# Small TensorE products that merge triangular inverses: order by head and then by block, two groups' 64-row steps alternating, and block transposes as 32x32 products

## The chip, the cores and the metric

The kernel runs on one core of a Trainium2 chip. The core has a matrix engine (TensorE, here PE, with its weight loads shown as a row of their own, PEld), a vector engine (VectorE, DVE), an engine for activations and copies (ScalarE, ACT), a general engine (GpSimd, POOL) and an engine that issues most of the transfers (SyncE, SP). The engines run their own instruction lists and wait for each other by semaphores. Matrix products are written to PSUM, the accumulators' memory; everything else lies in SBUF. The metric is the device time of one execution in microseconds; the median of three executions is given.

## The reference

Two decoder layers on 256 tokens of width 1024, all in float32. Each layer is a gated feed-forward part, a token mixer and a second feed-forward part, each between two RMS normalisations and added to the stream. The mixer runs a gated delta rule (8 heads of width 128, chunks of 64 tokens) beside a causal convolution of 31 taps. What matters here is the delta rule's triangular system:

```python
kk = jnp.einsum("bhncd,bhnsd->bhncs", k, k)
a_mat = jnp.where(strict, kk * decay * beta[..., :, None], 0.0)
lhs = jnp.eye(CHUNK, dtype=jnp.float32) + a_mat
rhs = jnp.concatenate([v * beta[..., None], k * (beta * jnp.exp(G))[..., None]], axis=-1)
sol = lax.linalg.triangular_solve(lhs, rhs, left_side=True, lower=True, unit_diagonal=True)
```

`lhs` is unit triangular. The kernel does not solve with it, it forms its inverse (over blocks of 128 tokens, so two blocks for each of 8 heads) and multiplies.

## The kernel before, in words

**Large products.** Every dense product is done in three parts, high·high, high·low and low·high, from weights that are split on the chip: a piece of weights is loaded into `raw` (four buffers), ACT rounds it to `whi` and DVE or POOL subtracts to get `wlo` (eight buffers each). These products write `mm` and make up most of PE's list. They come as a stream with the names `mm<-whi,xt`, `mm<-wlo,xt`, `mm<-whi,xt`.

**What sets the order.** PE's list is the order in which the program is written. Inside the mixer's projection a planner (`Lanes`) counts ticks of three or six large products each; small jobs (generators that yield between their steps) are put between the large products when their delay, in ticks, is over (`DELAY`, one number for each step of a job; the last one is used for all that follow). The planner also keeps a rough clock for PE, DVE and POOL, and gives a `wlo` subtraction to POOL or to DVE by those clocks. So a job with one step fewer, or with products of another counted cost, can move what comes behind it.

**The merge.** The inverse is built in blocks of 32 rows: POOL works out the inverses of the four 32x32 diagonal blocks of each matrix by substitution (`inverse`), transfers bring them into `U` (tile `u`). The job `merge` then puts the blocks together. A tile `u` or `at` holds 8 matrices of 128x128, 4 heads times 2 token blocks (the index `th`); there are two groups of heads (`gp` 1 and 0), so 16 matrices in all. The steps, with a yield after each:

- T, four times: four transposes of 128x128 into one PSUM tile, then three ACT copies of diagonal 32x32 blocks into `at`.
- A, for each group: 8 products of 32x32 for block 0, then 8 for block 64.
- B, for each group: 8 for block 0 and 8 for block 64 (named `gd<-u,at`), then 8 more for rows 32 to 64 (`gd<-at,u`).
- C, for each group: 8 products of 64x64 that contract over rows 0 to 64 and write rows 64 to 128 (`gd<-at`).
- D, for each group: 8 products of 64x64 that contract over rows 64 to 128 and write rows 0 to 64 (`gd<-u,at`).

Behind each step ACT copies the result to SBUF, and a later step waits for that copy. In every step six or nine large products stand between one block of small ones and the next. When `merge` is done the scan (`scan_first`, blocks `gd<-vr,u` and on) may begin. All small float32 products appear in the trace as two passes, each a weight load and a product; a 128x128 transpose is one pass. The trace's line L144 is the helper that issues products, L150 the one that issues transposes, L171 all of ACT, L124 all of DVE and POOL.

**Which rows a product uses.** PE's array takes the contracted rows from the partitions where the operands lie, and writes the partitions where the output lies. In A the two blocks use rows 0 to 32 with output 32 to 64, and rows 64 to 96 with output 96 to 128. In B they use rows 32 to 64 with output 0 to 32, rows 96 to 128 with output 64 to 96, and for the third kind rows 32 to 64 with output 32 to 64.

Of the kernel before, what the change touches and what calls it, by code (L numbers as in the profile page):

```python
# [12 lines left out]
AF = mybir.ActivationFunctionType  # L13
ALU = mybir.AluOpType

P = 128
# [315 lines left out]
def trunk(ctx: ExitStack, tc: tile.TileContext, x_in, wfirst, consts, feat, pch, tokp,  # L332
# [29 lines left out]
    def ps_gd(shape=None):  # L362
        return psum.tile(shape or [P, 4, P], F32, name="gd", tag="tr", bufs=3)
# [3 lines left out]
    T = Products(nc.tensor)  # L367
    V, S, W = Clocked(nc.vector, vector_us), Held(nc.scalar, T), Clocked(nc.gpsimd, pool_us)
# [29 lines left out]
    ident = cst[:, K_ID:K_ID + P]  # L398
# [345 lines left out]
    def mixer(xt, l, after_mix):  # L744
# [214 lines left out]
        AT = [None, None]  # L959
        U = [None, None]  # L960
# [62 lines left out]
        def merge():  # L1023
            ps = [None, None]
            for gp in (1, 0):
                at = AT[gp]
                for tb in range(2):
                    ts = slice(tb * 4, tb * 4 + 4)
                    pt = ps_gd()
                    for hl in range(4):  # L1030
                        T.transpose(pt[:, hl, :], U[gp][:, tb * 4 + hl, :], ident)
                    for b in (0, 64, 32):
                        S.copy(at[b:b + 32, ts, b:b + 32], pt[b:b + 32, :, b:b + 32])
                    yield
            for gp in (1, 0):
                at, ps[gp] = AT[gp], ps_gd([P, 16, 32])
                for b in (0, 64):
                    for th in range(8):
                        T.matmul(ps[gp][b + 32:b + 64, th, :], at[b:b + 32, th, b + 32:b + 64], at[b:b + 32, th, b:b + 32],
                                 start=True, stop=True)  # L1040
                for b in (0, 64):
                    S.copy(at[b + 32:b + 64, :, b:b + 32], ps[gp][b + 32:b + 64, 0:8, :])
                W.memset(at[0:32, :, 32:64], 0.0)
                yield
            for gp in (1, 0):
                at, u, p = AT[gp], U[gp], ps[gp]
                for b in (0, 64):
                    for th in range(8):
                        T.matmul(p[b:b + 32, 8 + th, :], at[b + 32:b + 64, th, b:b + 32], u[b + 32:b + 64, th, b + 32:b + 64],
                                 start=True, stop=True)  # L1050
                for th in range(8):
                    T.matmul(p[32:64, 8 + th, :], u[32:64, th, 32:64], at[32:64, th, 0:32], start=True, stop=True)
                for b in (0, 64):
                    S.activation(u[b:b + 32, :, b + 32:b + 64], p[b:b + 32, 8:16, :], AF.Copy, scale=-1.0)
                S.activation(at[32:64, :, 0:32], p[32:64, 8:16, :], AF.Copy, scale=-1.0)
                yield
            for gp in (1, 0):
                at, ps[gp] = AT[gp], ps_gd([P, 8, 64])
                for th in range(8):
                    T.matmul(ps[gp][64:128, th, :], at[0:64, th, 64:128], at[0:64, th, 0:64], start=True, stop=True)  # L1060
                S.copy(at[64:128, :, 0:64], ps[gp][64:128])
                yield
            for gp in (1, 0):
                at, u = AT[gp], U[gp]
                for th in range(8):
                    T.matmul(ps[gp][0:64, th, :], at[64:128, th, 0:64], u[64:128, th, 64:128], start=True, stop=True)
                S.activation(u[0:64, :, 64:128], ps[gp][0:64], AF.Copy, scale=-1.0)
                yield

        vr = [None, None]  # L1070

# [144 lines left out]
        def take(c):  # L1216
# [17 lines left out]

        acts = {
            "f": take, "decays": lambda c: decays(), "dts": lambda c: decay_pairs(), "inv": lambda c: inverse(), "merge": lambda c: merge(),
            "qs": lambda c: q_scale(), "cn": lambda c: conv_norm(), "cn1": lambda c: conv_out(1), "on": lambda c: o_norm(), "on0": lambda c: o_first(),
            "s0": lambda c: scan_first(), "s1": lambda c: scan_second(),
# [268 lines left out]
```

## Time and profile before

| | |
|---|---|
| median of 3 executions | 1353.26 us (1352.9 to 1353.55) |
| profiled execution, first to last instruction | 1349.7 us, so 3.56 us less than the median |
| PE busy | 98% of the span |
| granted TensorE clock | 0.999 |
| merge in layer 1, first to last small block | 352.3 to 381.5 us |
| merge in layer 2 | 1019.7 to 1049.2 us |

A row of the timeline gives the start, the time from the first start to the last end, the engine, the line, the operation, the tiles it writes and reads, and how many instructions were merged into the row. A matmul's end is modelled, and matmuls overlap, so what a block takes is read from starts: from the last large product ahead of it to the second large product behind it (the first one behind a block starts early and its successor is late), less two steps of the large products' pace.

### The profile page before, as it was taken

The numbers are of one execution on the slowest core, as the hardware profiler recorded it, in microseconds if no ns is written. First come the engines' busy times: TensorE is split into PE (matmuls) and PEld (weight loads), VectorE is DVE, ScalarE is ACT, GpSimd is POOL, SyncE is SP. The second block draws the span as 40 slices with busy tenths as digits, with TensorE's granted clock in tenths as the row PEclk, the third lists the DMA queues.
The fourth block names the chain that finished last, engine by engine and source line by source line (L and its number), as shares of the span: only waits on it lengthen the run. The fifth ranks groups of instructions, "written<-read, shape, count | busy, mean of one in ns | idle before, by whom it ended". The sixth has DMA issues, their size and how long they took to land.

```text
span 1349.7 us, 20220 instructions
## 1 busy us (share of the span) xinstructions
PE 1327.1 (98%) x7259; PEld 1128.0 (84%) x7259; DVE 933.8 (69%) x1594; ACT 732.3 (54%) x1175; POOL 445.5 (33%) x374
## 2 busy tenths in 40 slices
PE   9999999999999999999999999999999999999998
PEld 7888889997787888888888888899977878888886
DVE  6676455999966776665576654579999666766553
ACT  7545447675555545544455543577656564555541
POOL 0111017798744201111011120277986431011110
PEclk9999999999999999999999999999999999999999
DMA  8878746562634666776468775465545446477861
GB/s 274 287 239 260 249 156 210 166 211 96 206 110 153 225 218 222 276 249 221 155 219 280 265 235 186 146 231 172 173 138 183 143 139 234 154 261 247 273 212 39
DMA packets 115652, 273.76 MB, mean 203 GB/s; under 512 B 24768, under 2 KB 48352, under 8 KB 115552
## 3 DMA queue, kind: packets, MB, share of 16 engines
q1 hardware_dynamic: 115264, 272.40, 61.5%
q8 instruction: 57, 0.93, 0.3%
q14 instruction: 43, 0.35, 0.1%
q10 hardware_dynamic: 288, 0.07, 0.0%
HBM read 256.68 MB, written 15.75 MB: 202 GB/s over the span
## 4 chain that ended last, share of the span: by engine, by line
PE 81%; DVE 11%; ACT 3%; DMA 2%; issue 1%; POOL 1%; DVEq 0%; POOLq 0%; SPq 0%; ACTq 0%
PE mm L144 75%; DVE cacc L124 4%; PE gd L144 3%; DVE c L124 3%; DVE wlo L124 2%; PE tr L150 2%; DMA raw<-mw 2%; ACT whi L171 1%; DVE at L124 1%; ACT dt L171 1%; ACT sg L171 0%; DMA raw<-w2i 0%; DVE ssk L124 0%; DVE qk L124 0%; POOL rk L124 0%
## 5 line engine op out<-in xcount | busy, mean ns | idle before, releaser
L144 PE MATMUL mm<-whi,xt 128*128 128x512 f32 (+1 forms) x2048 | 647.6, 391 | 3.0 <-ACT qT L171 2.2
L171 ACT CAST whi<-raw 128x1024 fp32r<-128x1024 f32 (+2 forms) x448 | 458.8, 1035 | 316.8 <-PE mm L144 173.8
L124 DVE TENSOR_TENSOR wlo<-raw,whi 128x1024 fp32r<-128x1024 f32 (+2 forms) x342 | 427.2, 1264 | 190.0 <-ACT whi L171 183.5
L144 PEld LDWEIGHTS mm<-whi,xt 128*128 128x128 f32 x2048 | 382.3, 188 | 82.3 <-ACT qT L171 3.0
L144 PE MATMUL mm<-wlo,xt 128*128 128x512 f32 (+1 forms) x1024 | 396.4, 387 | 0.1
L124 POOL TENSOR_TENSOR wlo<-raw,whi 128x1024 fp32r<-128x1024 f32 (+1 forms) x106 | 250.5, 2379 | 142.5 <-ACT whi L171 140.0
L144 PEld LDWEIGHTS mm<-wlo,xt 128*128 128x128 f32 x1024 | 192.6, 188 | 37.6 <-DVE wlo L124 1.3
L144 PE MATMUL mm<-whi,act 128*128 128x512 f32 x704 | 218.3, 390 | 0.0
L124 POOL TENSOR_TENSOR act<-way,act 128x512 fp32r<-128x512 f32 x44 | 79.1, 1798 | 396.1 <-ACT act L171 385.9
L124 DVE SCALAR_TENSOR_TENSOR cacc<-hT,pc,cacc 128x254 f32<-128x254 f32 (+28 forms) x464 | 179.5, 472 | 0.2
L144 PE MATMUL mm<-xt,whi 128*128 128x256 f32 x960 | 175.5, 285 | 0.8 <-ACT qT L171 0.6
L144 PEld LDWEIGHTS mm<-whi,act 128*128 128x128 f32 x704 | 132.2, 188 | 27.4
L144 PEld LDWEIGHTS mm<-xt,whi 128*128 128x128 f32 x960 | 149.4, 192 | 1.9 <-ACT qT L171 0.9
L144 PE MATMUL mm<-wlo,act 128*128 128x512 f32 x352 | 137.0, 389 | 0.0
L144 PE MATMUL mm<-xt,wlo 128*128 128x256 f32 x480 | 135.9, 283 | 0.0
L171 ACT ACTIVATE ag<-mm,rstd 128x256 f32<-128x256 f32 x88 | 41.7, 474 | 100.0 <-PE mm L144 80.5
L144 PEld LDWEIGHTS mm<-xt,wlo 128*128 128x128 f32 x480 | 92.0, 192 | 0.0
L124 DVE SCALAR_TENSOR_TENSOR ag<-mm,rstd,ag 128x256 f32<-128x256 f32 x88 | 42.3, 481 | 58.7 <-ACT ag L171 58.4
L144 PEld LDWEIGHTS mm<-wlo,act 128*128 128x128 f32 x352 | 66.1, 188 | 13.6
L124 POOL TENSOR_TENSOR rpost<-ss,exp 128x1 f32<-128x1 f32 x12 | 6.5, 538 | 193.8 <-DVE ss L124 193.8
L171 ACT ACTIVATE jk<-mm 128x512 f32<-128x512 f32 x24 | 14.3, 598 | 60.4 <-PE mm L144 60.4
L124 DVE SCALAR_TENSOR_TENSOR c<-mm,pc,c 128x255 f32<-128x255 f32 (+2 forms) x108 | 43.7, 478 | 2.6 <-ACT c L171 2.6
(187 smaller groups left out, 1148.3 us busy)
## 6 DMA issues: line engine op xcount, KB each, us to landing
raw<-mw SPq DMA_DIRECT2D x168, 512.0 KB, 3.8
raw<-w2i SPq DMA_DIRECT2D x88, 512.0 KB, 4.8
raw<-w1i SPq DMA_DIRECT2D x84, 512.0 KB, 4.9
raw<-w1o SPq DMA_DIRECT2D x44, 512.0 KB, 4.7
raw<-w2o SPq DMA_DIRECT2D x44, 512.0 KB, 4.3
way<-way SPq DMA_DIRECT2D x176, 64.0 KB, 1.8
way<-way SPq DMA_DIRECT2D x44, 256.0 KB, 4.8
wbc<-feat SPq DMA_DIRECT2D x13, 512.0 KB, 4.9
```

The lines of the kernel that those rows point to most:

```text
L124: r = op(out, *a, **k)
L144: r = self.eng.matmul(o, w, x, **k)
L150: r = self.eng.transpose(*a)
L171: r = op(*a, **k)
```

## The change

Three edits in `merge`, nothing else:

- T: the four 128x128 transposes of a step become twelve products of a 32x32 diagonal block with the 32x32 identity (`gd<-cst,u`, line 144 now). The blocks are 0, 64 and 32 for each head in turn. The fourth diagonal block was never copied, and isn't made any more.
- A and B: the loops are swapped, so that for each matrix the products of all blocks follow each other; in B the third kind goes into the same loop.
- C and D: group 1's C stands alone as before. Group 0's C and group 1's D become one step in which their products alternate, followed by both ACT copies; group 0's D stands alone. Four steps become three.

```diff
                     for hl in range(4):
-                        T.transpose(pt[:, hl, :], U[gp][:, tb * 4 + hl, :], ident)
+                        for b in (0, 64, 32):
+                            bs = slice(b, b + 32)
+                            T.matmul(pt[bs, hl, bs], U[gp][bs, tb * 4 + hl, bs], ident[bs, bs], start=True, stop=True)
...
-                for b in (0, 64):
-                    for th in range(8):
+                for th in range(8):
+                    for b in (0, 64):
                         T.matmul(ps[gp][b + 32:b + 64, th, :], at[b:b + 32, th, b + 32:b + 64], at[b:b + 32, th, b:b + 32],
                                  start=True, stop=True)
...
-                for b in (0, 64):
-                    for th in range(8):
+                for th in range(8):
+                    for b in (0, 64):
                         T.matmul(p[b:b + 32, 8 + th, :], at[b + 32:b + 64, th, b:b + 32], u[b + 32:b + 64, th, b + 32:b + 64],
                                  start=True, stop=True)
-                for th in range(8):
                     T.matmul(p[32:64, 8 + th, :], u[32:64, th, 32:64], at[32:64, th, 0:32], start=True, stop=True)
...
-            for gp in (1, 0):
-                at, ps[gp] = AT[gp], ps_gd([P, 8, 64])
-                for th in range(8):
-                    T.matmul(ps[gp][64:128, th, :], at[0:64, th, 64:128], at[0:64, th, 0:64], start=True, stop=True)
-                S.copy(at[64:128, :, 0:64], ps[gp][64:128])
-                yield
-            for gp in (1, 0):
-                at, u = AT[gp], U[gp]
-                for th in range(8):
-                    T.matmul(ps[gp][0:64, th, :], at[64:128, th, 0:64], u[64:128, th, 64:128], start=True, stop=True)
-                S.activation(u[0:64, :, 64:128], ps[gp][0:64], AF.Copy, scale=-1.0)
-                yield
+
+            def inner(gp, th):
+                T.matmul(ps[gp][64:128, th, :], AT[gp][0:64, th, 64:128], AT[gp][0:64, th, 0:64], start=True, stop=True)
+
+            def outer(gp, th):
+                T.matmul(ps[gp][0:64, th, :], AT[gp][64:128, th, 0:64], U[gp][64:128, th, 64:128], start=True, stop=True)
+
+            ps[1] = ps_gd([P, 8, 64])
+            for th in range(8):
+                inner(1, th)
+            S.copy(AT[1][64:128, :, 0:64], ps[1][64:128])
+            yield
+            ps[0] = ps_gd([P, 8, 64])
+            for th in range(8):
+                inner(0, th)
+                outer(1, th)
+            S.copy(AT[0][64:128, :, 0:64], ps[0][64:128])
+            S.activation(U[1][0:64, :, 64:128], ps[1][0:64], AF.Copy, scale=-1.0)
+            yield
+            for th in range(8):
+                outer(0, th)
+            S.activation(U[0][0:64, :, 64:128], ps[0][0:64], AF.Copy, scale=-1.0)
+            yield
```

How the rows on PE moved is shown at three places; a count behind a row is how many instructions stand there. First a T step of layer 1, PE's list before:

```order
L144 MATMUL mm<-whi,xt 128x512
L150 MATMUL gd<-cst,u 128x128 x4
L144 MATMUL mm<-whi,xt 128x512
L144 MATMUL mm<-wlo,xt 128x512
L144 MATMUL mm<-whi,xt 128x512 x2
```

and now:

```order
L144 MATMUL mm<-whi,xt 128x512
L144 MATMUL gd<-cst,u 32x32 x12
L144 MATMUL mm<-whi,xt 128x512
L144 MATMUL mm<-wlo,xt 128x512
L144 MATMUL mm<-whi,xt 128x512 x2
```

Twelve small products stand where four transposes stood; the large products around them are the same. Second, step B of group 1, PE's list before:

```order
L144 MATMUL mm<-whi,xt 128x512
L144 MATMUL gd<-u,at 32x32 x16
L144 MATMUL gd<-at,u 32x32 x8
L144 MATMUL mm<-whi,xt 128x512
L144 MATMUL mm<-wlo,xt 128x512
```

and now (the first two of eight matrices):

```order
L144 MATMUL mm<-whi,xt 128x512
L144 MATMUL gd<-u,at 32x32 x2
L144 MATMUL gd<-at,u 32x32
L144 MATMUL gd<-u,at 32x32 x2
L144 MATMUL gd<-at,u 32x32
```

The 24 products are the same and stand between the same large products; only their order differs. Third, group 0's C and group 1's D on PE, before:

```order
L144 MATMUL gd<-at 64x64 x8
L144 MATMUL mm<-whi,xt 128x512
L144 MATMUL mm<-wlo,xt 128x512
L144 MATMUL mm<-whi,xt 128x512 x2
L144 MATMUL mm<-wlo,xt 128x512
L144 MATMUL mm<-whi,xt 128x512
L144 MATMUL gd<-u,at 64x64 x8
```

and now (the first two of eight pairs, and the large product ahead of them):

```order
L144 MATMUL mm<-whi,xt 128x512
L144 MATMUL gd<-at 64x64
L144 MATMUL gd<-u,at 64x64
L144 MATMUL gd<-at 64x64
L144 MATMUL gd<-u,at 64x64
```

The six large products that stood between the two blocks now come after the pair, so all that follows `merge` stands six large products earlier in PE's list, up to the transposes of the convolution's result, where the six come back. The planner also gives one `wlo` subtraction of each layer, near the merge, to POOL instead of DVE; ACT's list has the same instructions with some casts and copies exchanged.

## The prediction

> **What bounds the kernel now.** I read the page first, then the chain of waits around the merge, then PE's timeline there.
>
> ```profile
> span 1349.7 us, 20220 instructions
> PE 1327.1 (98%) x7259; PEld 1128.0 (84%) x7259; DVE 933.8 (69%) x1594; ACT 732.3 (54%) x1175; POOL 445.5 (33%) x374
> PE 81%; DVE 11%; ACT 3%; DMA 2%; issue 1%; POOL 1%; DVEq 0%; POOLq 0%; SPq 0%; ACTq 0%
> ```
>
> PE is busy nearly always and makes up 81% of the chain that ends last. In layer 1 the chain from the first transposes of the merge to well behind the scan is PE alone:
>
> ```profile
> 352.32 0.66 PE gd L150 x4
> ...
> 407.31 2.73 PE mm L144 x12
> ```
>
> All pieces between these two, too, are PE's small blocks and large products in turn. So here what a block of small products takes from PE is what it adds to the time, until a stall further on swallows it. The chain does not say how long a block takes by itself, so I read prices from the timeline's starts.
>
> **The pace and the price of each block.** A T step:
>
> ```profile
> 354.67 0.40 PE L144 MATMUL mm<-whi,xt 128*128 128x512 f32 x1
> 354.90 0.60 PE L150 MATMUL gd<-cst,u 128*128 128x128 f32 x4
> 355.26 0.48 PE L144 MATMUL mm<-whi,xt 128*128 128x512 f32 x1
> 355.57 0.39 PE L144 MATMUL mm<-wlo,xt 128*128 128x512 f32 x1
> 355.81 0.61 PE L144 MATMUL mm<-whi,xt 128*128 128x512 f32 x2
> 356.26 0.39 PE L144 MATMUL mm<-wlo,xt 128*128 128x512 f32 x1
> ```
>
> Three large products take 356.26 - 355.57 = 0.69, so 0.23 each. From the large product ahead to the second behind: 355.57 - 354.67 = 0.90, less two paces 0.46: **T costs 0.44**. Step A of group 1:
>
> ```profile
> 360.15 0.40 PE L144 MATMUL mm<-whi,xt 128*128 128x512 f32 x1
> 360.48 1.09 PE L144 MATMUL gd<-at 32*32 32x32 f32 x32
> 361.50 0.50 PE L144 MATMUL mm<-whi,xt 128*128 128x512 f32 x1
> 361.83 0.40 PE L144 MATMUL mm<-wlo,xt 128*128 128x512 f32 x1
> ```
>
> and of the view of the tile `gd`, with the least, median and greatest duration in ns:
>
> ```profile
> L144 PE MATMUL gd<-at x192: 191/191/267, 360.5 to 1043.7; 32*32 32x32 f32 x128, 64*64 64x64 f32 x64
> ```
>
> 1.68 - 0.46: **A costs 1.22**. That row (all products named so) gives 0.19 for one pass's own duration, so the 32 passes' starts cover 1.09 - 0.19 = 0.90, and 0.32 of the price is getting into the block and out of it. Step B of group 1 is the row that decides most:
>
> ```profile
> 366.07 0.40 PE L144 MATMUL mm<-whi,xt 128*128 128x512 f32 x1
> 366.40 1.00 PE L144 MATMUL gd<-u,at 32*32 32x32 f32 x29
> 367.21 0.21 PE L144 MATMUL gd<-at,u 32*32 32x32 f32 x1
> 367.24 0.19 PE L144 MATMUL gd<-u,at 32*32 32x32 f32 x1
> 367.26 0.19 PE L144 MATMUL gd<-at,u 32*32 32x32 f32 x1
> 367.27 0.19 PE L144 MATMUL gd<-u,at 32*32 32x32 f32 x1
> 367.29 0.19 PE L144 MATMUL gd<-at,u 32*32 32x32 f32 x1
> 367.30 0.19 PE L144 MATMUL gd<-u,at 32*32 32x32 f32 x1
> 367.32 0.57 PE L144 MATMUL gd<-at,u 32*32 32x32 f32 x13
> 368.17 0.40 PE L144 MATMUL mm<-wlo,xt 128*128 128x512 f32 x1
> ```
>
> 2.10 - 0.46: **B costs 1.64**. The thirteen passes at the end start every (0.57 - 0.19) / 12 = 0.032: one place of the array takes a pass every 0.032. But where the kind changes, the first `at,u` passes start while three `u,at` passes are still to come, and for that stretch the two kinds run side by side, each near its own 0.03, eight starts in 0.11. The second kind's late passes use rows 96 to 128, the third kind's rows 32 to 64. So products on different rows of the array do run together, even when they write the same tile `gd`; but only the few that stand near each other in the list, and block order puts such neighbours together only where one block ends. The new order makes every neighbour such a pair. The 64-row steps, C of group 1:
>
> ```profile
> 372.11 0.39 PE L144 MATMUL mm<-whi,xt 128*128 128x512 f32 x1
> 372.42 1.14 PE L144 MATMUL gd<-at 64*64 64x64 f32 x16
> 373.50 0.50 PE L144 MATMUL mm<-whi,xt 128*128 128x512 f32 x1
> 373.83 0.39 PE L144 MATMUL mm<-wlo,xt 128*128 128x512 f32 x1
> ```
>
> and its passes in the view of the tile `at`:
>
> ```profile
> L144 PE MATMUL gd<-at x16: 218/218/267, 372.4 to 373.3; 64*64 64x64 f32 x16
> ```
>
> 1.72 - 0.46: **C, and D like it, cost 1.26**. With 0.22 for a pass, the starts cover 1.14 - 0.22 = 0.92, that is 0.061 a pass, and 0.34 is entry and exit.
>
> **The change, part by part.** I take it that places on different rows run side by side at their own paces, and that two places on the same 32 rows take turns.
>
> A (four blocks): two places of 16 passes. 15 x 0.032 = 0.48, some 0.03 for the second's late start, 0.32 for entry and exit: 0.83 in place of 1.22. Saves 0.39 x 4 = **1.6**.
>
> B (four blocks): first and third kind both use rows 32 to 64, so 32 passes in a row, 31 x 0.032 = 0.99, plus 0.32: 1.31 in place of 1.64, the kind on rows 96 to 128 hidden beside them. Saves 0.33 x 4 = **1.3**. Whether the same rows with different outputs really take turns no row shows, since no block before has them next to each other. Side by side it would be 0.48 + 0.06 + 0.32 = 0.86, a saving of 3.1; if they take turns with everything, a loss (below). I take turns, since they draw their moving data from the same partitions.
>
> C and D (one pair per layer): rows 0 to 64 beside rows 64 to 128, and different PSUM tiles. 0.92 + 0.03 + 0.34 = 1.29 for the pair in place of 2.52. Saves 1.23 x 2 = **2.5**. No 64-row pair stands in the trace; it is bounded by the 32-row pair (full overlap) and by 31 x 0.061 + 0.34 = 2.23 (none), a saving of 0.6 in all. The pair waits for ACT's copy of group 1's C, which before ended well ahead of that place:
>
> ```profile
> 373.60 0.58 ACT L171 COPY at<-gd 64x512 f32<-64x512 f32 x1 [0.42 <-PE gd L144]
> 375.09 1.14 PE L144 MATMUL gd<-at 64*64 64x64 f32 x16
> ```
>
> 0.9 to spare, and the six large products between are kept.
>
> T (eight blocks): 12 products are 24 passes on three places with rows and outputs all different, 8 each: 7 x 0.032 = 0.22, 0.06 for the third's late start, and now a 32-row block's 0.32 for entry and exit: 0.60 in place of 0.44. Loses 0.16 x 8 = **1.3**. Bounds: with no late start 0.54, a loss of 0.8; with all 24 passes in turn 23 x 0.032 + 0.32 = 1.06, a loss of 5.0. I take the low part, by the overlapped rows of B. Part of it is covered: in layer 2 the third T step waits for ACT's copies of the first, which ACT begins late for its own reasons.
>
> ```profile
> 1023.55 0.79 ACT L171 COPY at<-gd 32x128 f32<-32x128 f32 x3
> 1023.91 0.40 PE L144 MATMUL mm<-whi,xt 128*128 128x512 f32 x1
> 1024.40 0.66 PE L150 MATMUL gd<-cst,u 128*128 128x128 f32 x4
> ```
>
> The wait is 0.49 - 0.23 = 0.26; two T steps ahead of it that are longer by 0.16 each use it up. So T loses 1.3 - 0.3 = **1.0**.
>
> The `wlo` moved to POOL, and the rest of the planner's shifts: nothing. POOL's 2.4 more (the second row below is one such subtraction) push its clearing of `at` to about 365.6 in layer 1, wanted by C at 372.42, and POOL idles 3.7 soon after:
>
> ```profile
> 363.18 0.30 POOL L124 MEMSET at<- 32x256 f32 x1
> 373.25 2.38 POOL L124 TENSOR_TENSOR wlo<-raw,whi 128x1024 fp32r<-128x1024 f32 x1 [3.73 <-ACT whi L171]
> ```
>
> Without that cover PE would wait out up to 2.4 a layer. The scan's blocks come six large products earlier, but each still has its old distance to the one ahead. The next PE stall is in the convolution's tail,
>
> ```profile
> 418.46 0.60 ACT L171 ACTIVATE gate<-mm 128x512 f32<-128x512 f32 x1 [0.31 <-PE mm L144]
> ...
> 422.81 0.66 PE L150 MATMUL tr<-cst,xhat 128*128 128x128 f32 x4 [1.72 <-ACT cf L171]
> ```
>
> and ACT's row of work ahead of it starts from a product of PE, so it moves with PE and swallows nothing.
>
> **Sum:** -1.6 - 1.3 - 2.5 + 1.0 = -4.4. The profiled execution's 1349.7 becomes 1345.3; the runs' median lies 3.56 above that execution, so 1353.26 becomes **1348.9**.
>
> **Two rules against the change.** Between the start of B's block and the first pass of its third kind lie 32 passes in 367.21 - 366.40 = 0.81, 0.025 each, which can be read as a limit on handing out passes. The Trainium skill, "TensorE: Matmul & The Clock Gate", section "Wait — 56ns, not 53.3ns?", says start-to-start never goes below about 25 ns however small the product. The eight starts in 0.11 above go below it, so the trace speaks against it for different places; it is the third rival. The Trainium skill, "TensorEngine Tiling (Array Packing)", section "Restrictions and Gotchas", says different row tiles can't use one PSUM bank at the same time; the overlapped rows write the same `gd` tile, so the trace disagrees, and by that rule the sum would be the slower rival's.
>
> **Rivals.**
>
> *All places run side by side, the same rows too* (25%): B saves 3.1 and not 1.3, so -6.2: 1347.1. For it: outputs differ; against: shared input rows.
>
> *64-row halves don't overlap* (7%): C and D save 0.6, not 2.5: -2.5, 1350.8. Nothing but the lack of a row speaks for it.
>
> *A limit of 0.025 on every start* (13%): A 31 x 0.025 + 0.32 = 1.10, saves 0.5; B 47 x 0.025 + 0.32 = 1.50, saves 0.6; C and D still 2.5; T 23 x 0.025 + 0.32 = 0.90, loses 3.7 - 0.3 = 3.4. Sum +0.2 saved: 1353.1, no change. For it: the 0.025 above; against: the eight starts.
>
> *Alternating breaks the overlap: the passes take turns* (10%, slower): the side-by-side stretch may be only a queue running empty, and one handing over after every product may not refill it. Then A 31 x 0.032 + 0.32 = 1.31, loses 0.4; B 47 x 0.032 + 0.32 = 1.82, loses 0.7; C and D save 0.6; T loses 5.0 - 0.3 = 4.7. Sum +5.2: 1358.5. It decides the sign once T's passes are slower than about 0.020 apart (0.020 x 23 + 0.32 is 0.78, a loss of 2.7 - 0.3) while A and B gain nothing and C and D their 2.5. Against it: both kinds keep their own pace while mixed.
>
> **Chances.** My forecast 45%. The measurement of this kernel tells about 0.2% (2.7 us) from no change. Faster: forecast 45, all side by side 25, half of the 64-row case: 74%. Same: the limit 13 and the other half: 16%. Slower 10%. The range takes in the first four: from 1346.3, 0.8 below the best case, to 1353.2.
>
> **What would show it.** T blocks with 24 passes in about 0.3 and a price near 0.6; A near 0.83; B near 1.31, where 0.86 would mean the second case; one pair near 1.3 with starts every 0.03; no wait of PE before the pair; PE's stall at the convolution's tail unchanged. I am wrong if T comes out at 0.9 or more, if the mixed starts are 0.025 or 0.032 apart, or if the blocks shrink and the scan or the stall behind it grows.

## The result

| | median | executions | 
|---|---|---|
| before | 1352.9 us (1350.82 to 1353.55) | 5 |
| the change | 1346.29 us (1344.52 to 1347.23) | 5 |

The ratio is 0.9956 with a 95% interval of 0.9944 to 0.9968: 6.6 us less by the medians, where 4.4 were forecast. In a later comparison the change stood at 0.9949 (0.9937 to 0.9962). The first lines of the page after:

```profile
span 1344.9 us, 20532 instructions
PE 1321.2 (98%) x7419; PEld 1120.4 (83%) x7419; DVE 931.6 (69%) x1592; ACT 731.8 (54%) x1175; POOL 451.2 (34%) x376
```

PE's instructions grew by 160, since eight T steps have 24 passes in place of four (8 x 20), and PE is as full as before. The profiled execution itself took 1346.66 us.

**The blocks after.** The rows answer to those shown of before, from PE's timeline of the change, and are read in the same way: from the large product ahead to the second one behind, less 0.46. A T step, layer 1:

```profile
355.58 0.39 PE L144 MATMUL mm<-whi,xt 128*128 128x512 f32 x1
355.90 0.45 PE L144 MATMUL gd<-cst,u 32*32 32x32 f32 x24
...
356.61 0.40 PE L144 MATMUL mm<-wlo,xt 128*128 128x512 f32 x1
```

1.03 - 0.46: T costs 0.57 where it cost 0.44. The 24 starts cover 0.45 - 0.19 = 0.26. Step A of group 1:

```profile
361.46 0.39 PE L144 MATMUL mm<-whi,xt 128*128 128x512 f32 x1
361.78 0.69 PE L144 MATMUL gd<-at 32*32 32x32 f32 x32
...
362.74 0.40 PE L144 MATMUL mm<-wlo,xt 128*128 128x512 f32 x1
```

1.28 - 0.46: A costs 0.82 (before 1.22). Step B of group 1, the row that matters:

```profile
366.55 0.39 PE L144 MATMUL mm<-whi,xt 128*128 128x512 f32 x1
366.87 0.22 PE L144 MATMUL gd<-u,at 32*32 32x32 f32 x2
366.89 0.21 PE L144 MATMUL gd<-at,u 32*32 32x32 f32 x1
366.93 0.20 PE L144 MATMUL gd<-u,at 32*32 32x32 f32 x2
366.94 0.19 PE L144 MATMUL gd<-at,u 32*32 32x32 f32 x1
...
367.38 0.19 PE L144 MATMUL gd<-at,u 32*32 32x32 f32 x1
...
367.84 0.40 PE L144 MATMUL mm<-wlo,xt 128*128 128x512 f32 x1
```

1.29 - 0.46: B costs 0.83 (before 1.64), no more than A, though it has half as many passes again. Its 48 passes start between 366.87 and 367.38, so 0.011 apart on average. The sixteen of the third kind (`gd<-at,u`) start between 366.89 and 367.38, one every 0.033, as close as passes of one place come when they stand alone. The third kind and one of the others use the same rows 32 to 64 of the array, and they don't take turns. The pair, group 0's C with group 1's D:

```profile
373.64 0.40 PE L144 MATMUL mm<-whi,xt 128*128 128x512 f32 x1
373.96 0.27 PE L144 MATMUL gd<-at 64*64 64x64 f32 x1
373.97 0.27 PE L144 MATMUL gd<-u,at 64*64 64x64 f32 x1
...
374.89 0.22 PE L144 MATMUL gd<-u,at 64*64 64x64 f32 x1
...
375.38 0.39 PE L144 MATMUL mm<-wlo,xt 128*128 128x512 f32 x1
```

1.74 - 0.46: the pair costs 1.28, where its two blocks cost 2.52 apart. 32 passes start in 374.89 - 373.96 = 0.93, and no row shows idle time ahead of them.

By these prices the change takes 0.40 x 4 (A) + 0.81 x 4 (B) + 1.24 x 2 (pair) = 7.3 away and adds 0.13 x 8 = 1.0 (T): 6.3 less. The medians say 6.6.

**The waits.** The profiled execution's span fell by 4.8 only. That is a matter of which executions were profiled. The span of before, 1349.7, is 3.2 under the median of 1352.9, while executions of that kernel in the later comparisons take 2.0 to 2.2 more than their spans; so its profile caught an execution some 1.1 faster than the median. The change's was 0.4 slower than its median, and its executions take 1.8 more than their spans, 0.3 less than those of before. Together that is the 1.8 between 4.8 and 6.6. Executions differ in their waits. In the view of what PE waited for (total us, times, longest), rows of after that differ:

```profile
PE tr L150 <- DMA x<-x: 0.7, 1, 0.7
...
PE mm L144 <- DVE ss L124: 0.7, 1, 0.7
PE mm L144 <- DVE xt L124: 0.6, 1, 0.6
...
PE gd L144 <- ACT sq L171: 0.4, 1, 0.4
```

and of before:

```profile
PE gd L150 <- ACT sq L171: 1.6, 2, 1.2
...
PE mm L144 <- DVE ss L124: 0.4, 1, 0.4
```

The waits for `x`, `ss` and `xt` came up in after. They lie far from the merge, as two of them show, one at the very start and one early in the first layer:

```profile
7.45 0.44 PE L150 MATMUL tr<-cst,x 128*128 128x128 f32 x2 [0.75 <-DMA x<-x]
...
194.10 0.74 PE L144 MATMUL mm<-whi,xt 128*128 128x512 f32 x2 [0.65 <-DVE xt L124]
```

Both come ahead of everything that was edited, so they are a matter of this execution, about a microsecond or two that one profile has and another hasn't. This is why the blocks were read one by one and the verdicts by medians. The wait for `sq` ahead of the first T step fell from 1.6 to 0.4 in these two profiles; it too moves from one execution to the next (1.0 in a second profile of the change), so no share of the gain is given to it.

The stall in the convolution's tail is what it was, 1.72 before the row of the transposes:

```profile
420.36 0.66 PE L150 MATMUL tr<-cst,xhat 128*128 128x128 f32 x4 [1.72 <-ACT cf L171]
```

### The profile page after: what moved, and what is told of

Its sections match the earlier page's. It is cut to its first block, busy times and chain, and to the rows that moved or that the text cites. A ratio compares the mean times of both kernels' runs of the same rounds, so it can differ in the third digit from the quotient of the medians.

```text
span 1344.9 us, 20532 instructions
## 1 busy us (share of the span) xinstructions
PE 1321.2 (98%) x7419; PEld 1120.4 (83%) x7419; DVE 931.6 (69%) x1592; ACT 731.8 (54%) x1175; POOL 451.2 (34%) x376
## 4 chain that ended last, share of the span: by engine, by line
PE 77%; DVE 10%; POOL 3%; ACT 3%; issue 3%; DMA 3%; SPq 0%; POOLq 0%; DVEq 0%; ACTq 0%
PE mm L144 72%; DVE cacc L124 3%; PE gd L144 3%; DVE c L124 3%; DVE wlo L124 2%; POOL wlo L124 2%; PE tr L150 2%; DMA raw<-mw 2%; ACT whi L171 1%; DVE at L124 1%; POOL rk L124 1%; ACT dt L171 1%; DMA raw<-w2i 0%; DMA x<-x 0%; DMA raw<-w1i 0%
## 5 line engine op out<-in xcount | busy, mean ns | idle before, releaser
L124 DVE TENSOR_TENSOR wlo<-raw,whi 128x1024 fp32r<-128x1024 f32 (+1 forms) x340 | 424.3, 1262 | 190.0 <-ACT whi L171 183.7
L124 POOL TENSOR_TENSOR wlo<-raw,whi 128x1024 fp32r<-128x1024 f32 (+1 forms) x108 | 254.1, 2371 | 143.7 <-ACT whi L171 142.9
```

The costliest lines, as they stand in the source:

```text
L124: r = op(out, *a, **k)
```

## The experiments

The theory after the result: each place of the array, a set of rows together with a set of output columns, takes a 32-row pass every 0.032 by itself, and different places run side by side, the same rows too; all that neighbours in the list must do is differ. The rivals: that one part of the change did all of the work, that the B gain came from rows 96 to 128 alone, or that a limit on handing out passes ends it soon.

### Each edit alone

Four kernels on one chip, with a median of before of 1351.81 us. The first is the change with the transposes kept:

```diff
                     for hl in range(4):
-                        for b in (0, 64, 32):
-                            bs = slice(b, b + 32)
-                            T.matmul(pt[bs, hl, bs], U[gp][bs, tb * 4 + hl, bs], ident[bs, bs], start=True, stop=True)
+                        T.transpose(pt[:, hl, :], U[gp][:, tb * 4 + hl, :], ident)
```

> The change without its first edit: the four 128x128 transposes of each T step stay, steps A to D are as in the change. If each place of the array (its rows and its output columns) works for itself, T's blocks go back from 0.57 to 0.44 each, eight times, 1.0 us less than the change has; up to 0.7 of it may be given back, since PE waits at the first and third T step for ACT. So 0.3 to 1.0 us under the change, about 7 us under the kernel before (ratio 0.9948). If the 32x32 turns gain something the prices do not show (a shorter wait for the transfers ahead of the first step), it is as slow as the change or slower.

Measured: 1343.71 us, 0.9945 (0.9929 to 0.996). Its T steps are back at 0.43 to 0.45 where PE did not wait, and the other blocks cost what they cost in the change. The ratio is the one that was expected, but its interval holds the change's 0.9956 too.

The second is the kernel before with this one edit only, the other way round.

> The kernel before with the first edit alone: 32x32 turns in place of transposes, steps A to D as before. Expected: T blocks at 0.57 in place of 0.44, eight times +1.0, of which the waits at the first and third step take back 0.3 to 0.7: +0.3 to +0.7 us, hard to tell from no change by the clock, plain in the prices. If the turns are a part of the gain, it is faster than before.

Measured: 1353.01 us, 1.0005 (0.9997 to 1.0014). A T step of it costs 0.58 in its timeline, as in the change. By price T alone adds 1.0; the interval of -0.4 to +1.9 us holds that and holds nothing at all too. The medians of the spans, 1351.2 beside 1349.75 of before, differ by some 1.4, since the time outside the span is 0.3 shorter in this kernel (about 1.8, before about 2.1); no run shows why. The waits that were expected to take a part of the price back did not: PE waited 2.5 for `sq` in its profile, beside 1.6 in that of before.

The third is the kernel before with the loops of A and B swapped:

```diff
-                for b in (0, 64):
-                    for th in range(8):
+                for th in range(8):
+                    for b in (0, 64):
                         T.matmul(ps[gp][b + 32:b + 64, th, :], at[b:b + 32, th, b + 32:b + 64], at[b:b + 32, th, b:b + 32],
...
-                for b in (0, 64):
-                    for th in range(8):
+                for th in range(8):
+                    for b in (0, 64):
                         T.matmul(p[b:b + 32, 8 + th, :], at[b + 32:b + 64, th, b:b + 32], u[b + 32:b + 64, th, b + 32:b + 64],
                                  start=True, stop=True)
-                for th in range(8):
                     T.matmul(p[32:64, 8 + th, :], u[32:64, th, 32:64], at[32:64, th, 0:32], start=True, stop=True)
```

> The kernel before with the second edit alone: steps A and B go by matrix and then by block; T, C and D as before. If each place works for itself: A 0.82 for 1.22 and B 0.82 for 1.63, four times each, -1.6 and -3.2, -4.8 us. If places on the same 32 rows take turns, as the forecast had it: B 1.31, -2.9 us. If all starts are at least 0.025 apart: -1.1 us.

Measured: 1348.11 us, 0.9971 (0.996 to 0.9982). The blocks cost 0.82 (A) and 0.82 to 0.84 (B) in its timeline, which is 4.8 by price; the median is 3.7 lower. The interval, 2.4 to 5.4 us, holds both.

The fourth is the kernel before with the third edit only (`inner`, `outer` and the pair, as in the diff of the change).

> The kernel before with the third edit alone: one group's C and the other group's D alternate; T, A and B as before. If the two 64-row halves work for themselves: one block of 1.28 for two of 1.27 in each layer, -2.5 us. If they take turns: 2.2 for 2.5, -0.6 us. The gain could also be less than the price if the scan, which comes six large products earlier, then waits for ACT or DVE.

Measured: 1349.29 us, 0.9981 (0.9973 to 0.999), so 1.4 to 3.6 us less; the pair costs 1.28 in it too, 2.5 by price.

What follows: within their intervals the three parts add up. T alone +0.7, A and B -3.9, C and D -2.6 by the ratios (ratio less one, times 1351.81) are -5.8 together; the change, run beside the next group of kernels, is -6.9 with an interval of 5.1 to 8.5 less. Most of it is A and B. That T gives a little back is shown by the prices; the ratios leave it open.

### The change again, and one block fewer

> The change itself once more, as the yardstick for the others on the same chip: 6 to 7 us under the kernel before (ratio near 0.9953), T blocks 0.57, A 0.82, B 0.82, the pair 1.28.

Measured: 1345.2 us, 0.9949 (0.9937 to 0.9962), before at 1351.73 us. The blocks cost what they cost in the first profile. The median of the spans is 1343.4 beside 1349.6 of before, 6.2 less, which is what the prices give; the medians of the times differ by 0.3 more, again by the time outside the span.

Beside it stood a kernel that keeps the transposes and puts group 0's A and group 1's B into one block, five places, so that a step's entry and exit are saved:

```diff
+            ps[0] = ps_gd([P, 16, 32])
+            for th in range(8):
+                first(0, th)
+                second(1, th)
+            first_out(0)
+            second_out(1)
+            yield
```

> The change without its first edit, and group 0's A goes into one block with group 1's B, product for product, as the change does with C and D; one step and one block fewer in each layer. The block has 80 passes on five places that differ in rows or in output columns. If each place works for itself at 0.032 and nothing else limits: the block costs 0.83, a whole block of 0.82 less in each layer, -1.6 us against the kernel without the first edit, about -8.5 us against the kernel before. If starts can't be closer than the 0.011 that B shows on three places: 79 x 0.011 + 0.32 = 1.19, -0.9 us. If the scan, six more products earlier, then waits for ACT, the gain is less than the prices.

Measured: 1343.67 us, 0.9937 (0.9924 to 0.9949). Neither expected price came. From PE's timeline of this kernel, the block and the one after it:

```profile
362.93 0.40 PE L144 MATMUL mm<-whi,xt 128*128 128x512 f32 x1
363.25 0.22 PE L144 MATMUL gd<-at 32*32 32x32 f32 x2
...
363.95 0.19 PE L144 MATMUL gd<-at,u 32*32 32x32 f32 x1
...
364.40 0.40 PE L144 MATMUL mm<-wlo,xt 128*128 128x512 f32 x1
...
365.33 0.40 PE L144 MATMUL mm<-whi,xt 128*128 128x512 f32 x1
366.04 0.22 PE L144 MATMUL gd<-u,at 32*32 32x32 f32 x2 [0.32 <-ACT at L171]
```

The block costs 364.40 - 362.93 - 0.46 = 1.01, with 80 passes in 0.70: 0.0089 each on average. A place has 16 passes, which at 0.032 would be 0.5; so with five places something else sets the pace of the block as a whole. Something else can be read here that the change did not have. One kind of A contracts over rows 0 to 32 and B's third kind over rows 32 to 64, and both write partitions 32 to 64 of their PSUM tiles. Their 32 passes in 0.70 are 0.023 apart, where turns would take 31 x 0.032 = 0.99. So the same output columns with other rows run side by side too. And the next block, group 0's B, now waits for ACT's copies of group 0's A, which were started late:

```profile
362.97 1.09 ACT L171 ACTIVATE gate<-mm 128x512 f32<-128x512 f32 x2
364.16 0.36 ACT L171 COPY at<-gd 32x256 f32<-32x256 f32 x1
364.55 1.05 ACT L171 CAST whi<-raw 128x1024 fp32r<-128x1024 f32 x1
365.62 0.36 ACT L171 COPY at<-gd 32x256 f32<-32x256 f32 x1
```

The second copy stands behind a cast of 1.05, ends at 365.98, and PE goes on at 366.04. That block costs 1.22 for 0.82. So of the 0.6 that one block fewer would save (0.82 + 0.82 - 1.01), 0.4 goes into the wait, in each layer.

The same kernel with three large products more ahead of group 0's B:

```diff
-    "merge": (4, 3, 2, 2, 2, 3, 2, 2),
+    "merge": (4, 3, 2, 2, 2, 3, 3, 2),
```

> The kernel that keeps the transposes and puts group 0's A and group 1's B into one block, with one tick of three large products more between that block and group 0's B, so that ACT's copies of group 0's A are finished when PE reaches B. My theory (a block costs what its busiest place or the hand-out of its passes takes, and the wait of 0.4 is all that B lost): the block stays at 1.01 to 1.02, B of group 0 falls from 1.216 to 0.82 and the idle time ahead of it is gone, so 0.8 less in all than with one tick fewer, 1342.9 by that run's median; a difference that only the prices can show. Rival: the third tick only moves the wait (the copies are late because ACT has a cast of whi and a gate activation ahead of them), and B stays at 1.2.

Measured: 1344.03 us, 0.9934 (0.9919 to 0.995), before at 1352.18 us. The wait is gone:

```profile
366.88 0.39 PE L144 MATMUL mm<-whi,xt 128*128 128x512 f32 x1
367.20 0.22 PE L144 MATMUL gd<-u,at 32*32 32x32 f32 x2
...
368.17 0.39 PE L144 MATMUL mm<-wlo,xt 128*128 128x512 f32 x1
```

1.29 - 0.46 = 0.83, and the block ahead of it is at 1.01 to 1.02 in both layers. The price falls by 0.8 as expected, and the median does not show it: the intervals of the two ratios overlap almost wholly. By price this is the cheapest of all these kernels, 0.6 x 2 below the change without its T edit; no measurement here tells the three versions without the T edit from each other.

### How far runs of one place can be, and what same rows cost

One kernel, with several variants of the order inside it (`one(k, th)` is the product of kind k for matrix th), of which one execution was profiled (1346.09 us); it was made for its block prices, not for its time:

```diff
-                for th in range(8):
-                    for b in (0, 64):
+                run = 2 if gp else 4
+                for b, th in [(b, t0 + t) for t0 in range(0, 8, run) for b in (0, 64) for t in range(run)]:
                         T.matmul(ps[gp][b + 32:b + 64, th, :], at[b:b + 32, th, b + 32:b + 64], at[b:b + 32, th, b:b + 32],
...
+                for pair, rest in [((0, 2), 1) if gp else ((0, 1), 2)]:
+                    for th in range(8):
+                        for k in pair:
+                            one(k, th)
+                    for th in range(8):
+                        one(rest, th)
```

> The change with four steps rearranged, to be read from the block prices of both layers, not from the time. (1) Group 1's A alternates its two places after 2 matrices (4 passes), group 0's after 4 (8 passes); before it was 8 matrices (1.22), in the change 1 (0.82). If three waiting passes ahead are reached, 4-pass runs still overlap nearly fully (0.8 to 0.9), 8-pass runs overlap by 3 of 8 (3 x 5 x 0.032 + 8 x 0.032 + 0.32 = 1.06). If any alternation is enough, both are 0.82; if only next neighbours overlap, both are above 1.0. (2) Group 1's B pairs the two kinds that share rows 32 to 64 and leaves the third kind for last: side by side 16 x 0.032 + 13 x 0.032 + 0.32 = 1.25; taking turns 32 x 0.032 + 13 x 0.032 + 0.32 = 1.76. (3) Group 0's B pairs the two kinds on different rows: 1.25 by all. (4) Group 1's T turns a fourth block, which nothing reads (work added, no result changed): with a place of its own 0.57 still; if starts are limited to 0.011, 31 x 0.011 + 0.32 = 0.66.

A of group 0 with four matrices of a block in a row, then B of group 1 (the two kinds on the same rows 32 to 64 paired, the kind on rows 96 to 128 last), then B of group 0 (two kinds on different rows paired), from PE's timeline of this kernel:

```profile
362.85 0.39 PE L144 MATMUL mm<-whi,xt 128*128 128x512 f32 x1
363.17 0.89 PE L144 MATMUL gd<-at 32*32 32x32 f32 x32
...
364.33 0.40 PE L144 MATMUL mm<-wlo,xt 128*128 128x512 f32 x1
...
365.25 0.39 PE L144 MATMUL mm<-whi,xt 128*128 128x512 f32 x1
...
366.94 0.40 PE L144 MATMUL mm<-wlo,xt 128*128 128x512 f32 x1
...
367.87 0.39 PE L144 MATMUL mm<-whi,xt 128*128 128x512 f32 x1
...
369.55 0.40 PE L144 MATMUL mm<-wlo,xt 128*128 128x512 f32 x1
```

B costs 1.69 - 0.46 = 1.23 with same rows paired and 1.68 - 0.46 = 1.22 with different rows paired. This settles the disputed cost: for two kinds that share their 32 rows and write different columns, sharing costs nothing. Turns would have given 1.76.

A costs 1.02 with runs of four matrices, 0.84 with runs of two (the other group), beside 0.82 with runs of one and 1.22 with runs of eight, the order before. Every place change lets the next place start about three passes early: one change of place takes 1.31 (the 32 passes in turn, 31 x 0.032 + 0.32) to 1.22, three take it to 1.02, 0.09 or three passes of 0.032 each. So about three passes can wait for their place while later ones go on. That is also what the rows of B before showed, where the first passes of the third kind started with three of the other kind to come. A fourth place in group 1's T steps, added in the same kernel, cost next to nothing: the step's 32 passes start within 0.26, 0.0084 apart, and it costs 0.58 to 0.59, where steps with three places cost 0.57 to 0.58.

### What limits five places

> The change with each T step made of 64 passes on eight places (the four diagonal blocks, and each block's rows once more with another output range, into a second PSUM tile; the second tile is read by nobody). In group 1's steps the eight places follow each other for each matrix; in group 0's steps each place gets two matrices, four passes, in a row. The question is what held five places at 0.0088 per pass. If PE hands out at most one pass every 0.0085 or so: both orders cover about 0.55 by their starts and cost 0.86. If PE only looks about 7 passes ahead: the first order the same 0.55, but the second has only two places in sight, 0.016 per pass, starts over 1.0 and a price near 1.3. If neither limits and five places were special, 8 passes a place at 0.032 give 0.26 and 0.57.

```diff
+                    places = [(b, d) for d in (0, 64) for b in (0, 64, 32, 96)]
+                    if gp:
+                        todo = [(hl, pl) for hl in range(4) for pl in places]
+                    else:
+                        todo = [(hl, pl) for h0 in (0, 2) for pl in places for hl in (h0, h0 + 1)]
+                    for hl, (b, d) in todo:
+                        bs, cs = slice(b, b + 32), slice((b + d) % 128, (b + d) % 128 + 32)
+                        T.matmul(pts[d // 64][cs, hl, bs], U[gp][bs, tb * 4 + hl, bs], ident[bs, bs], start=True, stop=True)
```

One execution was profiled (1358.47 us, some 6 more than before). In each layer group 1's first step stops for 2.73 ahead of the first pass that writes the second PSUM tile, and what follows runs at a low clock, so only steps at a granted clock of 1.00 are read: one of group 1's in layer 2, and one of group 0's next to it:

```profile
1031.47 0.75 PE L144 MATMUL gd<-cst,u 32*32 32x32 f32 x64
...
1033.72 0.85 PE L144 MATMUL gd<-cst,u 32*32 32x32 f32 x64
```

With the places in turn the 64 starts cover 0.75 - 0.19 = 0.56, or 0.0089 each on average, the same as for five places. With each place twice in a row they cover 0.66, or 0.0105 (0.66 in both steps of group 0 in layer 1 too). So a cost of five places in particular falls. A limit that hands out one pass every 0.009 would fit these averages, but the trace does not show one, for each block has a fast stretch and a slow one. The timeline cut off behind the first 32 passes of these two blocks says:

```profile
1031.47 0.35 PE L144 MATMUL gd<-cst,u 32*32 32x32 f32 x32
...
1033.72 0.40 PE L144 MATMUL gd<-cst,u 32*32 32x32 f32 x32
```

The first 32 passes start within 0.35 - 0.19 = 0.16 and 0.40 - 0.19 = 0.21, so 0.005 and 0.007 apart; the other 32 take 0.40 and 0.45 more. The block of five places has the same break. Two starts of B's third kind early in it, and two later ones:

```profile
363.43 0.19 PE L144 MATMUL gd<-at,u 32*32 32x32 f32 x1
...
363.46 0.19 PE L144 MATMUL gd<-at,u 32*32 32x32 f32 x1
...
363.65 0.21 PE L144 MATMUL gd<-at,u 32*32 32x32 f32 x1
...
363.70 0.19 PE L144 MATMUL gd<-at,u 32*32 32x32 f32 x1
```

Up to 363.46, with some 30 passes started, each of the five places gets its pass every 0.03, as in the change; from 363.65 to 363.81 four steps of this kind take 0.16, so 0.04 each. So five places do run side by side at full pace at first, and after some 32 passes of a block the pace falls. B of the change, 48 passes 0.011 apart, shows no such break. What sets the pace behind the break is open. If only two places were ever in sight in the second order, its passes would start 0.016 apart; its first 32 at 0.007 speak against that. How passes that wait are counted, for each place or in all, was not tried.

## Why the prediction was right, and where it was off

**Direction, mechanism and sum.** The time fell, by passes on different places running side by side once neighbours in the list differ. The rows of B before, eight starts in 0.11, were enough to see that, and the exits and entries of 0.32 and 0.34 read from before carried over. The median, 1346.29 us, lies at the very low end of the range, 1346.3, since one term was too small. That the range reaches so far is owed to the rival that had all places side by side: the forecast itself, 4.4 less, is 2.2 short of the measured 6.6, of which B makes 1.9.

**A:** forecast 0.83, measured 0.82. **C and D:** forecast 1.29 for the pair, measured 1.28, and PE did not wait ahead of it: ACT's copy of group 1's C ended well before, as the step said.

**B is the step that failed:** "two places on the same 32 rows take turns". It gave 1.31 and 1.3 us saved; measured were 0.83 and 3.2. The rival that has all places run side by side, the same rows too, had 0.86 and a total of 6.2 less, beside 6.3 by prices now; the mechanism of this rival is the one that the runs bear out. The reason I gave for turns, that they draw their moving data from the same partitions, has no row behind it, and the test that pairs just these two kinds (1.23 against 1.22) shows no cost of it. The rows of before couldn't decide it, because no two such products stood next to each other.

**T:** forecast 0.60, measured 0.57 to 0.58, so 1.0 and not 1.3 dearer in all eight blocks. 24 passes cover 0.26, 0.04 above the 0.22 of one place, where 0.06 stood for the late start of the last one. The other term, 0.3 that I let layer 2's third T step absorb, is not shown. That step has no wait left in the change: it costs 0.58, like the others. But three kernels that keep the transposes have none there either: with T kept, with A and B alone and with C and D alone the step costs 0.44, while the two kernels with A beside B have 0.78 and 0.60, and before had 0.76. So the wait comes and goes without longer T steps, and that they used it up can't be told.

**The limit of 0.025 per start** is refuted by B's 0.011 and by the 0.005 of eight places. It also rested on a miscount: by 367.21 only 29 of the 32 passes ahead of the third kind had started, as the row `x29` says, and 28 steps in 0.81 are 0.029, near one place's own pace. The Trainium skill, "TensorE: Matmul & The Clock Gate", section "Wait — 56ns, not 53.3ns?", has about 25 ns as the least distance of two starts; that fits passes of one place (0.032) and not passes of different places. **The rival in which passes take turns once alternated** is refuted by all of A, B and the pair; the Trainium skill's "TensorEngine Tiling (Array Packing)", section "Restrictions and Gotchas", on different row tiles in one PSUM bank speaks for that rival, and the three places of T, three row tiles writing one tile `gd` with starts 0.011 apart, disagree with it.

**The costs put at nothing** were nothing: POOL's one `wlo` more made no wait ahead of C, and the stall in the convolution's tail stayed at 1.72.

**Open:** the T edit's sign by time. By price it costs 1.0 us of the 7.3 that the other parts save, and the change without it has the lower median (1343.71 us, 0.9945 against 0.9949 for the change), but the intervals overlap. Also open is what slows a block of five or eight places after some 32 passes.

## What to carry to other kernels

Small float32 products on TensorE cost by place: put products that differ in rows or in output columns next to each other in the list, since only about three passes can wait for their place while others go on. The same rows with other columns are as good as other rows. Beyond four places there was little to gain here: five and eight places were faster for the first 32 passes or so, but over blocks of 80 and 64 passes they came to 0.009 a pass, no better than the 0.0084 of four places. Each such block between large products costs some 0.3 on top of its passes, so by price merging two blocks saves that much, as long as the copies behind them stay in time.

## What the runs showed of the hardware that was not expected

- Products on the same 32 rows with different output columns run side by side at full pace (B at 1.23 with the same and 1.22 with different rows).
- The same output columns with different rows run side by side too (32 passes 0.023 apart in the block with five places, where turns would be 0.032).
- On eight places the first 32 passes of a block start 0.005 apart, and the next 32 take 0.40; with five places the pace falls at about the same point. The averages over these blocks, 0.0089, are near the 0.0084 of four places; the cause of the break is open.
- In the kernel with eight places PE stood still for 2.73 inside the first T block of each layer, and the granted clock was half after it, for over 5 us in layer 1 and some 3 us in layer 2, with full busy time; the windows (stretch, length, PE busy, granted clock, DMA share, GB/s) show layer 1's beside a later one:

```profile
356.10:361.10 5.00, 5.00 (x86) 0.50 0.25 83
...
363.00:366.00 3.00, 3.00 (x135) 1.00 0.56 180
```

The stall of 1.72 in the convolution's tail, in the change, left the clock at 1.00. So a longer wait of PE can cost more than its own length, and a price read within such a stretch is not one of the operation. That the wait brings the low clock is argued from these two cases; no run changes it alone.
